# Attention blocks spread anew over the mixer's stages: more beside the first preparation and the middle stretch, fewer beside the chains

## The chip, the cores and the metric

One core of a Trainium2 chip runs the whole program. The metric is the device time of one execution in microseconds (us). Engines are named as in the profile: PE is TensorE's matmul stream and PEld its weight loads, DVE is VectorE, ACT is ScalarE, POOL is GpSimd, SP is SyncE, which issues DMAs; SPq is its queue.

## What is computed

One inference step of a two-layer backbone over 512 latent and 128 context tokens, 640 columns in all. Every layer is a SwiGLU, a token mixer and a second SwiGLU. What the change touches lies in the mixer of layer 0, which has two parts that do not depend on each other until the output projection:

```
p = h @ ab_w_in;  pa, pb = p[..., :ATTN_IN], p[..., ATTN_IN:]
oa = attention_mixer(pa, ...)     # 8 query heads, 2 kv heads, softmax
ob = rwkv_mixer(pb, ...)          # RWKV-7, one scan per direction
y  = concat([oa, ob]) @ ab_w_out
```

The attention is 20 jobs: 4 query heads of each kv head times 5 blocks of 128 queries. The first four blocks are latent queries (640 keys), the fifth is the context's (128 keys). The RWKV part runs on four pairs of heads (i = 0 to 3). Its scan over time is written in chunks of 64 tokens, ten chunks in each direction, with the inverse of a triangular matrix for every chunk, so that a scan is a chain of ten steps of small matmuls.

## The kernel before, in words

All of it is float32. Activations lie with channels on the partitions and the 640 tokens along the free axis.

`rwkv_attention` (L676) holds the mixer's second half, between the input projection and the output projection. Its work comes from five kinds of Python generators, each of which emits some instructions and then yields:

- `rwkv_prep(i)` (L971): loads r, k and v of pair i from DRAM (`rw_r`, `rw_k`, `rw_v`, one buffer each for r and k), makes decay, keys and rates for both directions on ACT, DVE and POOL (scan L1007, `ar` L1031, `kd` L1025, `bk` L1037 and L1038, `rr` L1066), then the chunk matrices `am` (matmuls into `ps_A`, mask L1054) and transposes `bt`. Counted as 22 yields.
- `tri_inverse` (L1209): the inverses of the 64 x 64 triangles. Four diagonal blocks go through DRAM (`invd`, L1222, L1229) to a substitution of many small DVE instructions (L1244, L1248), come back (`invx`, L1253, L1258), and are joined by 64 x 64 matmuls into `ps_n`. Counted as 16.
- `rwkv_chain(i)` (L1071): the ten steps, with matmuls into `ps_c` and `ps_yr`; at the end the final state goes out by SP (L1178). It needs the inverse of pair i. The tile `uv` has one buffer, so chains run one after the other. Counted as 12.
- `rwkv_out(i)` (L1180): group norm and gate, then a store to `od`. Counted as 4.
- `attention()` (L897): the 20 jobs. A job is two half-jobs, one of each kv head (`att_block`, L933), and the generator yields after each, 40 times in all. A half-job is scores into `ps_wide` (L941, L942; L944 for context), a maximum (DVE L947, L948), an exponential with its sum (ACT L950), a reciprocal (DVE L951), a scaling (ACT L952), transposes into `ps_pt` (PE L959) and their copies (ACT L961). The second half-job of a job adds the product with the values (PE L84 into `ps_pt`), a copy (ACT L929) and a store by SP to `od` (L930). The queries of the next job are loaded by SP (L73, `att_qin`) as soon as the one before it begins.

A half-job is called a block here. Blocks 0 to 39 come in the order of the jobs; in each group of ten, the last two are context blocks with 128 keys, called short, and the others, called long, have 640.

The function `take(rounds, n, *gens)` mixes them: in each of its rounds it advances every generator by its count over the rounds, and then the attention so that n blocks have been emitted by the last round, evenly spread. The eight calls are the stages: stage 1 is preparation 0; stage 2 inverse 0 with preparation 1; stage 3 chain 0 with inverse 1; stage 4 chain 1, preparation 2 and out 0; stage 5 out 1, inverse 2 and preparation 3; stage 6 inverse 3 and chain 2; stage 7 out 2 and chain 3; stage 8 out 3.

What the emission order sets: the program is built with a planner (`TileContext(nc, schedule_with_timeline_sim=True)`) that fixes the order of instructions on every engine's queue and takes the order of emission as a priority. On the chip each queue then runs in that fixed order; an instruction that waits holds up everything behind it on its queue. The loads that go through `load` (L71) are kept in emission order on SP, where the stores `od`, `invd`, `invx` and the final states are issued too.

Of the kernel before, what the change touches and what calls it, by code (L numbers as in the profile page):

```python
# [31 lines left out]
class K:  # L32
# [643 lines left out]
    def rwkv_attention(self):  # L676


        att = self.attention()
        mset = self.nc.gpsimd.memset  # L680

        self.rt = [self.mixb.tile([128, 2, 128], F32, name=f"rt{k}") for k in range(2)]
        for t in self.rt:
            mset(t[64:, 0], 0.0)
            mset(t[:64, 1], 0.0)

        self.st = [self.mixb.tile([128, 2, 2, 64], F32, name=f"st{k}") for k in range(4)]
        for t in self.st:
            for h in range(2):
                mset(t[64 - 64 * h:128 - 64 * h, :, h], 0.0)  # L690

        self.dx = [self.mixe.tile([128, 20, 64], F32, name=f"inv_d{k}") for k in range(2)]
        mset(self.dx[1].rearrange("p i t -> p (i t)"), 0.0)
        self.invd = [self.dram.tile([2, 80, 256], F32, name=f"invd{k}") for k in range(2)]
        self.invx = [self.dram.tile([2, 2, 80, 256], F32, name=f"invx{k}") for k in range(2)]
        un = [{} for _ in range(4)]

        def take(rounds, n, *gens):

            gens = [[g, 0.0, c] for g, c in gens]  # L700
            total, done = rounds, 0
            for step in range(rounds):
                for g in gens:
                    g[1] += g[2] / rounds
                    while g[0] is not None and (g[1] >= 1 or step == rounds - 1):
                        g[1] -= 1
                        try:
                            next(g[0])
                        except StopIteration:
                            g[0] = None  # L710
                while done < n * (step + 1) // rounds:
                    next(att, None)
                    done += 1

        prep = lambda i: (self.rwkv_prep(i, un[i]), 22)
        inv = lambda i: (self.tri_inverse(un[i]), 16)
        chain = lambda i: (self.rwkv_chain(i, un[i]), 12)
        out = lambda i: (self.rwkv_out(i, un[i]), 4)
        take(28, 5, prep(0))
        take(16, 4, inv(0), prep(1))  # L720
        take(12, 8, chain(0), inv(1))
        take(10, 7, chain(1), prep(2), out(0))
        take(12, 9, out(1), inv(2), prep(3))
        take(12, 5, inv(3), chain(2))
        take(12, 2, out(2), chain(3))
        take(4, 0, out(3))
        for _ in att:
            pass
# [1237 lines left out]
```

## Time and profile before

| | us |
|---|---|
| median of 3 runs | 3218.09 |
| lowest and highest | 3214.31, 3220.37 |
| the profiled execution, its own time | 3211.53 |
| span of the profile (first to last instruction) | 3209.8 |
| mean granted clock of TensorE, share of full | 0.949 |

The span is what the rows below are measured in, from its first instruction on. The mixer's stages lie between about 733 and 1237 us. The page's second part cuts the span into 40 slices of 80 us, one digit each, the busy share in tenths. Stages are cut in the trace by their own marks, for instance the last mask of `am` of a preparation or the store of a chain's final state.

### The profile page before, as it was taken

The numbers are of one execution on the slowest core, as the hardware profiler recorded it, in microseconds if no ns is written. First come the engines' busy times: TensorE is split into PE (matmuls) and PEld (weight loads), VectorE is DVE, ScalarE is ACT, GpSimd is POOL, SyncE is SP. The second block draws the span as 40 slices with busy tenths as digits, with TensorE's granted clock in tenths as the row PEclk, the third lists the DMA queues.
The fourth block names the chain that finished last, engine by engine and source line by source line (L and its number), as shares of the span: only waits on it lengthen the run. The fifth ranks groups of instructions, "written<-read, shape, count | busy, mean of one in ns | idle before, by whom it ended". The sixth has DMA issues, their size and how long they took to land.

```text
span 3209.8 us, 57218 instructions
## 1 busy us (share of the span) xinstructions
PE 2963.9 (92%) x23107; PEld 2763.7 (86%) x23107; DVE 1859.2 (58%) x3787; ACT 1182.7 (37%) x2443; POOL 694.7 (22%) x814
## 2 busy tenths in 40 slices
PE   7999999996888888999999999999987599999998
PEld 6999999884566667999999999999976499999998
DVE  5433348525656654854575876665678946633346
ACT  4422235424344434533333552222442245422223
POOL 1000005123112201533241322222223623000002
PEclk8999999997798898999999999999988899999998
DMA  6433335631111107354443454443478653432223
GB/s 225 139 132 119 109 104 183 214 128 45 18 29 33 21 14 194 108 168 138 152 150 124 139 174 148 148 153 109 139 154 242 240 178 100 162 108 79 69 90 112
DMA packets 370943, 408.55 MB, mean 127 GB/s; under 512 B 75258, under 2 KB 336695, under 8 KB 370423
## 3 DMA queue, kind: packets, MB, share of 16 engines
q1 hardware_dynamic: 356182, 365.93, 36.7%
q0 software_dynamic: 14496, 38.97, 4.2%
q8 instruction: 182, 2.98, 0.4%
q14 instruction: 83, 0.67, 0.1%
HBM read 358.79 MB, written 44.86 MB: 126 GB/s over the span
## 4 chain that ended last, share of the span: by engine, by line
PE 78%; DVE 8%; DMA 5%; POOL 3%; issue 3%; ACT 2%; SPq 1%; POOLq 0%; DVEq 0%; ACTq 0%
PE ps_h L439 10%; PE ps_h L440 10%; PE ps_h L441 10%; PE ps_wide L439 6%; PE ps_wide L440 6%; PE ps_wide L441 5%; PE ps_y L439 5%; PE ps_y L440 5%; PE ps_y L441 5%; PE ps_wide L274 2%; PE ps_n L84 1%; DVE s5x L1630 1%; PE ps_in L441 1%; PE ps_in L439 1%; PE ps_in L440 1%
## 5 line engine op out<-in xcount | busy, mean ns | idle before, releaser
L412 DVE TENSOR_TENSOR wlo<-w,whi 128x1024 fp32r<-128x1024 f32 (+2 forms) x574 | 574.9, 1008 | 387.9 <-ACT whi L411 380.7
L411 ACT CAST whi<-w 128x1024 fp32r<-128x1024 f32 (+2 forms) x576 | 482.9, 846 | 847.7 <-PE ps_h L440 277.7
L439 PE MATMUL ps_h<-hh,whi 128*128 128x320 f32 x2112 | 657.8, 312 | 6.5 <-ACT hh L356 2.4
L440 PE MATMUL ps_h<-hl,whi 128*128 128x320 f32 x2112 | 656.1, 311 | 0.3 <-DVE hl L357 0.3
L441 PE MATMUL ps_h<-hh,wlo 128*128 128x320 f32 x2112 | 655.3, 311 | 0.0
L439 PEld LDWEIGHTS ps_h<-hh,whi 128*128 128x128 f32 x2112 | 398.7, 189 | 13.2 <-ACT whi L411 4.5
L440 PEld LDWEIGHTS ps_h<-hl,whi 128*128 128x128 f32 x2112 | 398.1, 189 | 2.6 <-issue 1.5
L441 PEld LDWEIGHTS ps_h<-hh,wlo 128*128 128x128 f32 x2112 | 397.9, 188 | 1.2 <-issue 0.8
L440 PE MATMUL ps_y<-gl,whi 128*128 128x320 f32 x1056 | 325.9, 310 | 0.1
L441 PE MATMUL ps_y<-gh,wlo 128*128 128x320 f32 x1056 | 325.4, 310 | 0.0
L439 PE MATMUL ps_y<-gh,whi 128*128 128x320 f32 x1056 | 323.7, 311 | 1.4 <-ACT y L530 1.4
L439 PE MATMUL ps_wide<-hh,whi 128*128 128x320 f32 x912 | 288.6, 316 | 7.6 <-ACT pm L771 1.9
L440 PE MATMUL ps_wide<-hl,whi 128*128 128x320 f32 x912 | 285.9, 313 | 0.0
L441 PE MATMUL ps_wide<-hh,wlo 128*128 128x320 f32 x912 | 285.1, 313 | 0.4 <-DVE wlo L412 0.4
L373 POOL TENSOR_TENSOR ssy<-ssy,sq 128x320 f32<-128x320 f32 x84 | 95.5, 1137 | 559.2 <-ACT sq L372 556.7
L439 PEld LDWEIGHTS ps_y<-gh,whi 128*128 128x128 f32 x1056 | 197.1, 188 | 6.8 <-ACT y L530 2.5
L440 PEld LDWEIGHTS ps_y<-gl,whi 128*128 128x128 f32 x1056 | 198.2, 188 | 1.1 <-issue 0.5
L441 PEld LDWEIGHTS ps_y<-gh,wlo 128*128 128x128 f32 x1056 | 198.0, 188 | 1.1 <-issue 0.8
L439 PEld LDWEIGHTS ps_wide<-hh,whi 128*128 128x128 f32 x912 | 173.9, 191 | 15.3 <-issue 5.3
L481 DVE SCALAR_TENSOR_TENSOR g<-th,ps_h 128x320 f32<-128x320 f32 x159 | 77.1, 485 | 174.6 <-PE ps_h L441 174.1
L440 PEld LDWEIGHTS ps_wide<-hl,whi 128*128 128x128 f32 x912 | 173.3, 190 | 1.5 <-issue 0.9
L441 PEld LDWEIGHTS ps_wide<-hh,wlo 128*128 128x128 f32 x912 | 173.2, 190 | 1.0 <-DVE wlo L412 0.6
(464 smaller groups left out, 5588.0 us busy)
## 6 DMA issues: line engine op xcount, KB each, us to landing
w<-in_ffn_w_dram SPq DMA_DIRECT2D x120, 1024.0 KB
ada_w<-in_ada_w_dram SPq DMA_DIRECT2D x72, 1024.0 KB
w<-in_ffn_w_dram SPq DMA_DIRECT2D x112, 512.0 KB
w<-in_ab_w_in_dram SPq DMA_DIRECT2D x14, 1024.0 KB
s5cd<-s_work POOLq DMA_DIRECT2D x128, 64.0 KB, 2.4
s5bd<-s_st POOLq DMA_DIRECT2D x32, 256.0 KB, 3.5
s5bt<-s5bd SPq DMA_DIRECT2D x32, 256.0 KB
w<-in_s_w_out_dram SPq DMA_DIRECT2D x8, 1024.0 KB
```

The lines of the kernel that those rows point to most:

```text
L84: i = self.nc.tensor.matmul(**p).ins
L274: nc.tensor.matmul(ps[32 * g:32 * g + 32, :256], self.sc[:, 2 * t + k, :], w[:, k, g * 256:g * 256 + 256], start=(t + k == 0), stop=(2 * t ...
L373: nc.gpsimd.tensor_tensor(ss, ss, sq, op=OP.add)
L411: a = self.nc.scalar.copy(hi[:, :kt], s)
L412: v = (eng or self.nc.vector).tensor_tensor(lo[:, :kt], s, hi[:, :kt].bitcast(F32), op=OP.subtract)
L439: nc.tensor.matmul(o, hi[:, k], ah[k][half], start=(k == 0), stop=False)
L440: nc.tensor.matmul(o, hi[:, k], al[k][half], start=False, stop=False)
L441: self.last[0] = nc.tensor.matmul(o, lo[:, k], ah[k][half], start=False, stop=(k == kt - 1))
L481: nc.vector.scalar_tensor_tensor(g, t, 0.5, p3[:, :HALF], op0=OP.mult, op1=OP.mult)
L1630: V.tensor_tensor(dst, dst, t1, op=OP.add)
```

## The change

The second argument of seven `take` calls, which is the number of attention blocks emitted in that stage. The sum stays 40, and nothing else is edited.

```diff
-        take(28, 5, prep(0))
-        take(16, 4, inv(0), prep(1))
-        take(12, 8, chain(0), inv(1))
-        take(10, 7, chain(1), prep(2), out(0))
-        take(12, 9, out(1), inv(2), prep(3))
-        take(12, 5, inv(3), chain(2))
+        take(28, 8, prep(0))
+        take(16, 5, inv(0), prep(1))
+        take(12, 6, chain(0), inv(1))
+        take(10, 5, chain(1), prep(2), out(0))
+        take(12, 10, out(1), inv(2), prep(3))
+        take(12, 4, inv(3), chain(2))
         take(12, 2, out(2), chain(3))
         take(4, 0, out(3))
```

## Rows read from the trace of the kernel before

**Rows 1.** The page: its span, and PE's busy share in 40 slices of 80 us.

```profile
span 3209.8 us, 57218 instructions
...
PE   7999999996888888999999999999987599999998
```

**Rows 2.** Busy time by stage, stages 1 to 6, then 7 with 8 (PEclk: granted clock).

```profile
733.00:794.00 61.00, 42.83 (x228) 29.31 (x229) 33.61 (x56) 27.89 (x54) 18.46 (x11) 0.72 0.10 31
794.00:863.00 69.00, 53.52 (x533) 39.33 (x531) 47.90 (x125) 24.67 (x51) 17.55 (x10) 0.78 0.12 20
863.00:931.00 68.00, 57.86 (x894) 45.26 (x894) 39.73 (x144) 29.83 (x74) 5.30 (x4) 0.90 0.12 21
931.00:1018.00 87.00, 74.75 (x830) 56.92 (x827) 48.28 (x113) 39.29 (x98) 19.52 (x12) 0.86 0.11 34
1018.00:1111.00 93.00, 75.73 (x658) 55.84 (x655) 59.50 (x152) 40.08 (x86) 20.08 (x11) 0.82 0.13 27
1111.00:1176.00 65.00, 55.83 (x905) 45.10 (x904) 37.67 (x140) 23.10 (x62) 5.37 (x4) 0.87 0.11 18
1176.00:1237.00 61.00, 44.18 (x600) 33.41 (x600) 25.20 (x73) 22.80 (x59) 3.92 (x2) 0.88 0.24 66
```

**Rows 3.** The exponential's line L950 alone, stages 1 to 6; two instructions a block.

```profile
733.00:794.00 61.00, 5.88 (x12) 0.72 0.10 31
794.00:863.00 69.00, 3.09 (x8) 0.78 0.12 20
863.00:931.00 68.00, 7.50 (x15) 0.90 0.12 21
931.00:1018.00 87.00, 6.38 (x16) 0.86 0.11 34
1018.00:1111.00 93.00, 8.05 (x18) 0.82 0.13 27
1111.00:1176.00 65.00, 4.52 (x10) 0.87 0.11 18
```

**Rows 4.** The chain that ended last, from stage 3 into stage 4.

```profile
932.34 2.59 DMA out_dram<-s_out
...
937.02 3.21 DMA rw_k<-rwd
```

**Rows 5.** That chain by line, in stages 1, 3, 4, 5 and 6.

```profile
by line: PE ps_A L84 11.9%; PE ps_wide L941 10.4%; issue 7.2%; DVE ar L1031 7.0%; PE ps_pt L84 5.2%; DVE am L1054 4.8%; PE ps_w L849 4.3%; PE ps_bt L1059 3.8%; POOL kd L1040 3.4%; DVE bk L1037 3.3%; PE ps_hb L841 3.3%; POOL bk L1038 3.2%; P
...
by line: PE ps_n L84 12.8%; PE ps_pt L959 6.2%; DMA invd<-am 5.0%; DMA inv_d<-invx 4.9%; SPq L1258 4.5%; PE ps_wide L941 4.5%; PE ps_yr L1158 4.4%; DMA invx<-inv_x 4.0%; ACT att_p L950 3.9%; PE ps_c L1120 3.7%; DVE mx L947 3.5%; issue 3.4%;
...
by line: DMA rw_k<-rwd 7.6%; PE ps_A L84 7.5%; PE ps_wide L941 6.8%; PE ps_pt L84 4.4%; PE ps_hb L841 4.0%; DVE gi L1007 3.4%; PE ps_hs L822 3.4%; PE ps_bt L1059 3.4%; PE ps_yr L1158 3.2%; PE ps_pt L959 3.2%; PE ps_w L849 3.2%; DMA out_dram
...
by line: PE ps_n L84 11.7%; PE ps_A L84 8.6%; DVE am L1054 5.6%; PE ps_wide L941 4.5%; PE ps_pt L959 4.4%; DVE mx L947 4.4%; PE ps_w L849 4.2%; POOL am L1232 3.1%; PE ps_hb L841 3.1%; DVE inv_d L1283 2.8%; issue 2.8%; PE ps_pt L84 2.7%; SPq
...
by line: PE ps_n L84 22.3%; PE ps_yr L1158 5.9%; PE ps_pt L959 5.5%; PE ps_c L1145 4.5%; DMA invx<-inv_x 4.2%; PE ps_yr L1163 3.8%; DMA inv_a<-invd 3.5%; DMA inv_d<-invx 3.4%; DVE am L1283 3.4%; issue 3.2%; DVE inv_d L1283 3.2%; PE ps_c L11
```

**Rows 6.** Busy time summed over all stages, tiles ps_wide, att_p and pts.

```profile
sum 504.00, PE 53.06 PEld 27.09 DVE 28.66 ACT 35.99; mean PE 7.58 PEld 3.87 DVE 4.09 ACT 5.14
...
sum 504.00, PE 34.18 PEld 22.24 ACT 65.75; mean PE 4.88 PEld 3.18 ACT 9.39
...
sum 504.00, PE 26.67 PEld 21.68 ACT 27.08; mean PE 3.81 PEld 3.10 ACT 3.87
```

**Rows 7.** Timeline of stage 1: start, duration, instruction, idle before it and releaser.

```profile
780.91 1.23 PE L84 MATMUL ps_A<-ar,bk 64*128 64x128 f32 x8 [7.89 <-DVE bk L1037]
...
784.73 2.61 PE L84 MATMUL ps_A<-ar,bk 64*128 64x128 f32 x16
...
790.88 1.16 PE L84 MATMUL ps_A<-ar,bk 64*128 64x128 f32 x16
```

**Rows 8.** Waits on SP's queue, all stages: total us, times, longest.

```profile
SPq L930 <- ACT att_out L929: 110.0, 13, 22.3
```

## The prediction

> **What bounds the kernel now.** I read the page first. PE is busy nearly all the time outside the mixer of layer 0; the slices from 720 to 1280 us are the weak stretch, with digits of 6 to 9 [rows 1]. The change edits nothing outside that stretch, so the rest of the 3209.8 us span is taken as unchanged, and the whole question is what some 500 us do.
>
> The second view is the busy time by stage [rows 2]. Stages 1 and 2 leave PE idle most: 61 - 42.83 = 18.2 us and 69 - 53.52 = 15.5 us, and the granted clock is low there (0.72 and 0.78). Stages 3, 4 and 6, those with a chain, have PE busy for 85 to 86% at 0.86 to 0.90. Stage 5 is in between (81%, 0.82), with DVE at 59.50 of 93 us. No engine is full anywhere: each stage is a path of dependent steps that runs from engine to engine, with fixed queues, and attention is what stands between those steps.
>
> Do the blocks run where they are emitted? The exponential has two instructions a block, so the counts of its line are 6, 4, 7.5, 8, 9 and 5 blocks in stages 1 to 6 [rows 3], against 5, 4, 8, 7, 9 and 5 emitted. The planner stays within about one block of the emission. So the new numbers will be seen in the trace.
>
> Are the stages serial? The chain that ended last goes from the store of chain 0's final state (932.34, 2.59 us) to the load of preparation 2's k on the same queue (937.02, 3.21 us) [rows 4]. Preparation 2 can't start before chain 0 has ended. So a microsecond saved in stage 3 is passed on, and one lost in stage 1 too.
>
> **Which blocks move.** Emitted before, stage by stage: 0-4, 5-8, 9-16, 17-23, 24-32, 33-37, 38-39. After: 0-7, 8-12, 13-18, 19-23, 24-33, 34-37, 38-39. The short blocks are 8, 9, 18, 19, 28, 29, 38 and 39. Counted so, stage 1 gains three long blocks, stage 2 one short (it gives away 5, 6, 7 and receives 9 to 12), stage 3 loses two long, stage 4 one long and one short, stage 5 gains one long, stage 6 loses one long. Four long blocks and a short one leave the chains' stages and come into those without.
>
> **What a block is made of.** PE: 53.06 us of scores, 34.18 of transposes and 26.67 of products with the values, 113.9 us in all [rows 6]. With a short block counted as a quarter (an estimate: one key block of five, and fixed parts), these are 34 long ones, 3.35 us each. ACT: 65.75 + 27.08 = 92.8 us, 2.7 us each; DVE: 28.66 us, 0.84 each. A block also issues DMAs: each pair of blocks loads two query tiles and stores one `od` tile on SP. That queue has been held up by such stores for 110.0 us, 13 times [rows 8], mostly with nothing urgent behind them; a store that comes earlier stands ahead of preparation 1's loads and inverse 0's `invd`. POOL's queue has no instruction of a block.
>
> **What a block costs where it stands.** The bounds are nothing (all in idle time) and 3.35 us (all on the path). The nearest evidence between is the chain by line [rows 5], in which I add the attention's lines and divide by the blocks of the stage [rows 2, 3]:
>
> - Stage 1: 10.4 + 5.2 = 15.6% of 61 us is 9.5 us, over 6 blocks 1.6 us.
> - Stage 3: 6.2 + 4.5 + 3.9 + 3.5 = 18.1% of 68 us is 12.3 us, over 7.5 blocks 1.6 us.
> - Stage 4: 6.8 + 4.4 + 3.2 = 14.4% of 87 us is 12.5 us, over 8 blocks 1.6 us.
> - Stage 5: 4.5 + 4.4 + 4.4 + 2.7 = 16.0% of 93 us is 14.9 us, over 9 blocks 1.65 us.
> - Stage 6: 5.5% of 65 us is 3.6 us, over 5 blocks 0.7 us.
>
> The lines that the view cuts off are missing in all of them alike. A second witness: stages 3 and 6 hold the same other work, a chain and an inverse, and last 68 and 65 us with 7.5 and 5 blocks [rows 2, 3]; that is 1.2 us a block, inside the same bounds. I take the chain's prices, because they exist for every stage and the pair agrees within half a microsecond. Stage 2 takes stage 1's price, a quarter of it for a short block.
>
> **The sum.** Stage 1 +3 x 1.6 = +4.8; stage 2 +0.4; stage 3 -2 x 1.6 = -3.2; stage 4 -1.25 x 1.6 = -2.0; stage 5 +1.65; stage 6 -0.7. Together +0.9 us: the blocks cost about as much where they go as where they come from. The profiled execution took 3211.53 us, so 3212.4 by its measure; the median of the runs, 3218.09, stands 6.6 us above it, and I forecast 3219.0 by the median. A difference below 0.2%, some 6.4 us, is about what a measurement of this kernel can't tell from none.
>
> **Rival 1, faster: the idle time of stage 1 takes the blocks for nothing.** For it: PE waited 7.89 us in one piece before `ps_A` of the second direction [rows 7], with three blocks not yet emitted that would fill it (three long blocks are 10 us of PE against 18.2 us idle). And the 16 matmuls into `ps_A` right after took 2.61 us where the next 16 took 1.16 us; the granted clock was 0.72 over the stage, so much of it ran at the lower of the two levels, 1.2 GHz, after that wait. A filled gap gives back 1.45 us there. Beside chains a block is then worth its PE time times PE's busy share: stage 3 -2 x 2.85, stage 4 -1.25 x 2.9, stage 6 -2.9, stage 5 +2.7, stages 1 and 2 nothing but the -1.45. Sum -11 us: 3207. Against it: the queue of PE was in fixed order while it waited those 7.89 us, with a block's transposes standing behind `ps_A`; and during that wait DVE was the path, which blocks load too.
>
> **Rival 2, slower: in stage 1 the added blocks stand ahead of the path.** Preparation 0 is one chain of steps with nothing to overlap it but attention. If the queue order puts scores, transposes, maxima and stores ahead of ready steps, each block costs its whole 3.35 us in stages 1, 2 and 5 (+10, +0.8, +3.35), while stages 3, 4 and 6 return the pair's 1.2 us or less (-2.4, -1.5, -0.7): +9.5 us, 3227.6. It decides from about 3.0 us a block in stage 1 on: then the sum passes 6.4 us. For it: 15.6% of stage 1's chain is attention already. Against it: 1.6 us a block so far.
>
> **Rival 3, slower: the chains lose their fill and the clock.** With fewer blocks PE waits more between the steps of a chain, and runs its many small matmuls at the lower level. Stage 6, with 5 blocks, has 0.87 where stage 3 with 7.5 has 0.90, and stage 5 has 0.82 where stage 4 has 0.86 [rows 2, 3]. If stages 3 and 4 fall to those, 6% of 68 us and 8% of 87 us more run at half rate, and half of that is lost: 5.5 us, with the sum 6.4 us: 3224.5. The Trainium skill, page "TensorE: Matmul & The Clock Gate", section "Why this matters for your kernels", says to leave no idle gaps between bursts of matmuls, since PE falls to half rate; by that rule fill should not leave the chains, and equally should come into stage 1. The trace agrees for the gap in stage 1 [rows 7] and is thin for the chains, since five blocks cost stage 6 only 0.03 of clock.
>
> **Rival 4: the planner undoes it**, and blocks run where they ran. Then nothing changes. Rows 3 speak against it.
>
> **How the numbers follow.** Forecast 0.40, rival 1 0.30, rival 2 0.21, rival 3 0.06, rival 4 0.03. Faster is rival 1, 0.30; within 0.2% the forecast and rival 4, 0.43; slower rivals 2 and 3, 0.27. The range reaches from rival 1 less the 3 us by which runs differ, 3204, to rival 2 plus as much, 3231. Between cases of both signs the forecast's own range is 3212 to 3225.
>
> **What would show it.** Exponentials of about 8, 5, 6, 5, 10 and 4 blocks in stages 1 to 6. By the forecast stage 1 is 5 us longer than 61, stages 3 and 4 together some 5 us shorter than 155, stage 5 nearly 2 us longer than 93. Rival 1 leaves stage 1 at 61 or less, with a smaller wait before `ps_A` and a clock above 0.72. Rival 2 makes it over 70. Rival 3 shows in a clock under 0.87 in stage 3. I am wrong if the stages' differences don't add up to the change of the span, or if another part of the program moves by over 3 us.

## The result and the profile after

The change makes the kernel slower: a median of 3237.08 us (3236.42 to 3238.98, 4 runs) against 3218.39 us (4 runs), a ratio of 1.006 with the interval 1.0044 to 1.0076. That is 18.7 us, outside the forecast's range. The profiled execution after took 3238.98 us with a span of 3237.2 us, 27.4 us over the span of before [rows 1]. That is more than the medians show, because the profile of before was 6.9 us below its own median and this one 1.9 us above.

The page of the changed kernel, its span and PE's busy share in the 40 slices, answers to [rows 1]:

```profile
span 3237.2 us, 57222 instructions
...
PE   7999999997688787999999999999986689999998
```

The weak stretch is where it was. Next, busy time by stage, stages 1 to 6 and then 7 with 8, which answers to [rows 2] (columns: stretch, its length, busy time of PE, PEld, DVE, ACT and POOL, granted clock, DMA share, GB/s):

```profile
735.80:804.30 68.50, 51.76 (x271) 36.54 (x272) 37.22 (x65) 35.09 (x70) 18.85 (x11) 0.73 0.10 30
804.30:887.50 83.20, 55.16 (x543) 40.12 (x542) 51.65 (x129) 26.73 (x55) 18.89 (x10) 0.75 0.11 18
887.50:955.50 68.00, 55.07 (x892) 43.44 (x890) 36.10 (x140) 25.15 (x69) 5.35 (x4) 0.90 0.11 20
955.50:1039.90 84.40, 69.77 (x780) 52.93 (x781) 49.35 (x108) 35.67 (x84) 19.51 (x11) 0.86 0.11 33
1039.90:1136.70 96.80, 75.48 (x655) 54.57 (x655) 58.38 (x152) 42.24 (x89) 21.27 (x11) 0.81 0.12 26
1136.70:1197.20 60.50, 50.59 (x903) 40.43 (x901) 37.00 (x139) 21.22 (x58) 4.84 (x4) 0.94 0.12 19
1197.20:1260.20 63.00, 45.10 (x598) 34.11 (x599) 24.76 (x72) 22.40 (x58) 4.45 (x3) 0.83 0.24 63
```

Cut at the same marks to a tenth, the stages of before last 61.0, 69.2, 68.2, 88.2, 90.6, 65.9 and 60.5 us. So stage 1 grew by 7.5 us, **stage 2 by 14.0**, stage 5 by 6.2 and the last by 2.5; stage 3 gave 0.2 back, stage 4 3.8 and stage 6 5.4. Together +20.8 us. Stages 2 and 5 of the kernel before, at these marks:

```profile
793.80:863.00 69.20, 53.72 (x534) 39.46 (x532) 48.10 (x125) 24.67 (x51) 17.55 (x10) 0.78 0.12 20
...
1019.40:1110.00 90.60, 73.52 (x647) 54.41 (x646) 57.54 (x148) 39.47 (x84) 20.08 (x11) 0.81 0.13 27
```

In stage 2 PE is hardly busier (53.72 us before, 55.16 after). The 14 us are mostly waiting.

The stages' 20.8 us are not the 27.4 us of the span: 3.0 lie ahead of the mixer and 3.6 behind it, which the prediction named as a sign of being wrong. No edit touches the program there, and the stretch behind the mixer lasts from 1967 to 1980 us over the nineteen profiles. So 6.6 us are within what two profiles differ by, and say nothing of the change.

Did the blocks move as the diff says? The exponential's line alone, stages 1 to 6, answers to [rows 3] (columns: stretch, length, busy time of ACT with the count, two for a block):

```profile
735.80:804.30 68.50, 8.36 (x18) 0.73 0.10 30
804.30:887.50 83.20, 4.51 (x10) 0.75 0.11 18
887.50:955.50 68.00, 5.08 (x12) 0.90 0.11 20
955.50:1039.90 84.40, 4.91 (x10) 0.86 0.11 33
1039.90:1136.70 96.80, 9.04 (x20) 0.81 0.12 26
1136.70:1197.20 60.50, 3.53 (x8) 0.94 0.12 19
```

They did: 9, 5, 6, 5, 10 and 4 blocks. By kind, though, the blocks that ran differ from those emitted. Stage 1 has eight long and one short where it had six long, and stage 2 four long and one short where it had two of each.

In stage 1 the timeline of PE answers to [rows 7]:

```profile
787.65 2.07 PE L941 MATMUL ps_wide<-keys,att_qin 128*128 128x512 f32 x2 [5.85 <-ACT att_p L950]
...
790.08 2.24 PE L84 MATMUL ps_pt<-pts,vt 128*64 128x128 f32 x20
792.25 0.71 PE L84 MATMUL ps_A<-ar,bk 64*128 64x128 f32 x8
```

The wait of 7.89 us ahead of `ps_A` is gone; a block fills that place. But the block's own scores now wait 5.85 us for an exponential, and the stage as a whole is longer. On SP the stores held the queue nearly as before, as the waits of that queue show (columns: total us, times, longest), against [rows 8]:

```profile
SPq L930 <- ACT att_out L929: 117.1, 16, 22.8
```

What fills stage 2? PE's longest new wait there stands in front of the first joining matmul of inverse 0. The timeline of the kernel before shows the substitution that this matmul needs, and what came behind it (columns: start, duration, instruction, idle before it with its releaser):

```profile
799.53 0.17 DVE L1244 TENSOR_TENSOR inv_t<-inv_a,inv_x 80x14 f32<-80x14 f32 x1 [1.00 <-ACT inv_x L1237]
...
807.23 0.28 DVE L1248 TENSOR_TENSOR inv_x<-inv_x,inv_t 80x14 f32<-80x14 f32 x2
...
809.25 0.49 DVE L1005 TENSOR_SCALAR lw<-lw 128x640 f32<-128x640 f32 x1 [1.74 <-ACT lw L1004]
...
815.25 0.44 PE L84 MATMUL ps_n<-inv_d,am 64*64 64x64 f32 x2 [3.81 <-DMA inv_d<-invx]
```

The same stretch of the changed kernel:

```profile
809.93 0.17 DVE L1244 TENSOR_TENSOR inv_t<-inv_a,inv_x 80x14 f32<-80x14 f32 x1 [3.24 <-ACT inv_x L1237]
...
819.10 0.49 DVE L1005 TENSOR_SCALAR lw<-lw 128x640 f32<-128x640 f32 x1 [1.26 <-ACT lw L1004]
...
819.74 1.48 DVE L1007 TENSOR_TENSOR_SCAN gi<-reset,lw 128x640 f32<-128x640 f32 x1
...
823.14 0.16 DVE L951 RECIPROCAL mx<-mx 128x1 f32<-128x1 f32 x1 [1.02 <-ACT att_p L950]
...
823.81 2.31 POOL L1034 TENSOR_TENSOR ar<-rw_r,e 128x640 f32<-128x640 f32 x1 [11.60 <-ACT e L1014]
...
823.90 0.81 DVE L1031 SCALAR_TENSOR_TENSOR ar<-kkh,e 128x630 f32<-128x630 f32 x1
...
824.63 1.52 DVE L1244 TENSOR_TENSOR inv_t<-inv_a,inv_x 80x14 f32<-80x14 f32 x1
...
826.14 0.81 DVE L947 TENSOR_REDUCE mx<-ps_wide 128x1 f32<-128x640 f32 x1
...
826.88 0.16 DVE L1248 TENSOR_TENSOR inv_x<-inv_x,inv_t 80x14 f32<-80x14 f32 x1
...
834.31 0.44 PE L84 MATMUL ps_n<-inv_d,am 64*64 64x64 f32 x2 [8.65 <-DMA inv_d<-invx]
```

Read the substitution as one thing, from the first L1244 to the last L1248. Before, it ran from 799.53 to 807.51, 7.98 us, and preparation 1's `lw` and `gi` stood behind it. After, it runs from 809.93 to 827.04, 17.11 us, and `lw`, `gi`, `ar`, a block's reciprocal and maxima stand inside it, some of them waiting for ACT. It issues the same 56 instructions; the planner has put twelve others between them where there were four. The loads through DRAM follow from its end, so PE's wait grew from 3.81 to 8.65 us, and preparation 1's next `ps_A` matmuls stand behind that wait on PE's queue.

Inverse 2 in stage 5 has the same: its substitution lasts 18.29 us after, with fifteen others inside (12.48 us before, with nine), and PE's wait for it grew from 1.24 to 7.73 us:

```profile
1045.68 0.30 PE L84 MATMUL ps_n<-inv_d,am 64*64 64x64 f32 x2 [1.24 <-DMA inv_d<-invx]
...
1072.03 0.45 PE L84 MATMUL ps_n<-inv_d,am 64*64 64x64 f32 x2 [7.73 <-DMA inv_d<-invx]
```

### The profile page after: what moved, and what is told of

Its sections match the earlier page's. It is cut to its first block, busy times and chain, and to the rows that moved or that the text cites. A ratio compares the mean times of both kernels' runs of the same rounds, so it can differ in the third digit from the quotient of the medians.

```text
span 3237.2 us, 57222 instructions
## 1 busy us (share of the span) xinstructions
PE 2966.6 (92%) x23107; PEld 2765.3 (85%) x23107; DVE 1856.8 (57%) x3787; ACT 1185.6 (37%) x2445; POOL 696.0 (22%) x814
## 4 chain that ended last, share of the span: by engine, by line
PE 77%; DVE 9%; DMA 4%; POOL 3%; ACT 3%; issue 3%; SPq 1%; POOLq 0%; DVEq 0%; ACTq 0%
PE ps_h L439 10%; PE ps_h L440 10%; PE ps_h L441 10%; PE ps_wide L439 6%; PE ps_wide L440 6%; PE ps_wide L441 5%; PE ps_y L439 5%; PE ps_y L440 5%; PE ps_y L441 5%; PE ps_wide L274 2%; PE ps_n L84 1%; DVE s5x L1630 1%; POOL ssx L373 1%; PE ps_in L441 1%; PE ps_in L439 1%
```

## The experiments

**Theory A, order:** the loss comes from the substitutions being broken up on DVE's queue. **Theory B, weight:** it comes from what the added blocks themselves take in stages 1, 2 and 5. The table is the summary; the runs follow. Columns: ratio to the kernel before; length of stages 1, 2 and 5; length of the whole mixer; substitution of inverse 0 and of inverse 2 (first L1244 start to last L1248 end); PE's wait ahead of the first `ps_n` of inverse 0 and 2. Times in us; all columns but the ratio are read from one profile of each kernel, at the same marks. A ratio is against the kernel before run beside it; it need not be the quotient of two medians. A substitution is called whole where it lasts no more than 12.5 us, as both do in the kernel before, and broken where it lasts longer; what stands inside it differs by degrees.

| kernel | ratio | stage 1, 2, 5 | mixer | subst. 0, 2 | wait 0, 2 |
|---|---|---|---|---|---|
| before | 1 | 61.0, 69.2, 90.6 | 503.7 | 8.0, 12.5 | 3.8, 1.2 |
| changed | 1.0060 | 68.5, 83.2, 96.8 | 524.3 | 17.1, 18.3 | 8.7, 7.7 |
| e1_early | 1.0059 | 66.7, 86.9, 100.4 | 527.6 | 16.4, 18.1 | 8.6, 7.7 |
| e2_late | 1.0007 | 66.9, 70.2, 96.3 | 506.9 | 8.0, 12.2 | 3.9, 0 |
| e3_first | 1.0060 | 66.7, 81.6, 95.8 | 519.7 | 17.9, 17.1 | 15.1, 7.6 |
| e4_pin | 1.0060 | 68.7, 84.6, 95.5 | 523.9 | 13.1, 16.9 | 7.4, 7.6 |
| e5_behind | 1.0059 | 66.4, 77.8, 101.2 | 528.2 | 8.6, 23.6 | 1.1, 8.9 |
| e6_seven | 1.0031 | 63.0, 74.2, 91.5 | 505.4 | 8.1, 12.0 | 5.4, 0 |
| e7_four | 1.0010 | 58.2, 76.4, 91.5 | 513.8 | 12.1, 10.8 | 1.4, 4.1 |
| e8_second | 1.0024 | 61.0, 82.5, 97.1 | 513.6 | 8.0, 21.0 | 2.7, 9.7 |
| e9_behind02 | 1.0019 | 68.7, 78.3, 89.1 | 510.4 | 8.6, 11.9 | 1.1, 1.5 |
| e14_first_behind02 | 1.0004 | 68.4, 73.4, 86.3 | 510.2 | 8.7, 8.5 | 2.7, 1.5 |
| e15_behind2 | 1.0047 | 68.5, 88.8, 86.8 | 519.4 | 17.1, 8.4 | 8.7, 1.3 |
| e13_split | 0.9989 | 63.2, 79.4, 91.9 | 506.8 | 15.7, 10.7 | 7.3, 3.9 |
| e16_split2 | 1.0036 | 64.2, 69.7, 100.4 | 515.7 | 8.0, 17.6 | 4.0, 7.7 |
| e17_both | 1.0025 | 64.2, 76.9, 96.4 | 512.6 | 17.2, 17.2 | 7.8, 6.9 |
| e10_before_behind2 | 0.9989 | 63.2, 70.1, 88.4 | 503.8 | 8.0, 8.5 | 3.8, 0 |
| e11_chains | 0.9977 | 61.0, 69.3, 85.8 | 495.2 | 8.0, 8.0 | 3.9, 3.3 |
| e12_chains_behind2 | 0.9973 | 64.7, 69.5, 81.7 | 496.8 | 8.0, 8.0 | 3.8, 2.9 |

### Which part of the change

The first half alone (stages 1 to 4), the second half alone (stages 5 and 6), and three blocks moved from stage 2 to stage 1 with all else as before:

```diff
 e1_early: counts 8, 5, 6, 5, 9, 5, 2, 0
 e2_late:  counts 5, 4, 8, 7, 10, 4, 2, 0
 e3_first: counts 8, 1, 8, 7, 9, 5, 2, 0
```

> Block counts 8, 5, 6, 5, 9, 5, 2, 0: the change without its swap of one block between stages 5 and 6. Both theories put the loss into stages 1 and 2, where the trace after lost 7.5 and 14.0 us, and have stages 5 and 6 cancel (+6.0 and -5.4 us). Theory A (order: the inverse's substitution in stage 2 is broken up on DVE's queue) and theory B (weight: every block costs its work, about 3 us, outside the chains' stages, and nothing comes back beside chains): both 3234 to 3240, ratio 1.005 to 1.007. A ratio under 1.003 would say that the late swap is the cause.

> Block counts 5, 4, 8, 7, 10, 4, 2, 0: only the swap between stages 5 and 6. Both theories: within 2 us of before, 3216 to 3221, stage 5 some 3 to 6 us longer and stage 6 as much shorter. Slower by over 5 us would say that the late swap carries the loss.

> Block counts 8, 1, 8, 7, 9, 5, 2, 0: three blocks from stage 2 to stage 1, nothing else moved. Theory B (weight): stage 1 longer by 7 us, stage 2 shorter by about as much, since three blocks fewer stand there: total within 3 us of before. Theory A (order): stage 1 longer by 7 us; stage 2 depends on whether DVE's order still breaks up the substitution of inverse 0: if it does, the first matmul of the inverse comes 25 us after the diagonal blocks' landing instead of 16 us and the total is 8 to 16 us slower; if not, as theory B.

e1_early took 3234.14 us, ratio 1.0059 [1.004, 1.0078]: the whole loss. e2_late took 3217.77 us, 1.0007 [0.9994, 1.002]: none. e3_first took 3234.5 us, 1.006 [1.0043, 1.0077]: the whole loss again, though stages 1 and 2 together emit as many blocks as before and no chain loses one. The price that three blocks have in one stage rather than the next can hardly be 19 us when their PE work is 10; it needs a second mechanism.

### Mending the order in the changed kernel

First, preparation 1's `lw` and `gi` alone were put behind the substitution's last step:

```diff
-            nc.vector.tensor_scalar(lw, lw, 1.0, None, op0=OP.add)
-            gi = self.tmp("gi")
+            with (self.tc.issue_after(self.sub_last.ins) if (i, d) in ((1, 0),) else ExitStack()):
+                nc.vector.tensor_scalar(lw, lw, 1.0, None, op0=OP.add); gi = self.tmp("gi")
...
+                self.sub_last = nc.vector.tensor_tensor(x[:, d, s + 1:, :s], x[:, d, s + 1:, :s], t3, op=OP.add)
```

> The changed kernel, with the first scan of preparation 1 (its two DVE instructions, lw and gi) put behind the last step of inverse 0's substitution on DVE's queue. Theory A (order): the substitution ends some 8 us earlier after its start, as before the change, PE's wait of 8.65 us for the diagonal inverses shrinks to about 4, and 6 to 10 us come back: 3227 to 3231, ratio 1.003 to 1.004. Theory B (weight): the blocks in stage 2 cost what they cost, 3235 to 3239, ratio 1.005 to 1.007.

It took 3234.73 us, 1.006 [1.0037, 1.0083]. Theory A's expectation was missed, and the profile says why: the substitution still lasted 13.1 us, because a block's reciprocal, waiting for its exponential, and a maximum stood inside it. So all DVE work emitted after the substitution was queued behind its last step, first for inverse 0, then for inverses 0 and 2, later for inverse 2 alone:

```diff
-                            next(g[0])
+                            with queued(): next(g[0])
...
-                    next(att, None)
+                    with queued(): next(att, None)
...
+                self.sub_last = done if s == 14 and u["n"] in (0,) else self.sub_last; yield
```

Here `queued` is `issue_after` of the last L1248 step of the named inverse; e9_behind02 has `(0, 2)`, e15_behind2 `(2,)`, and e14_first_behind02 is e3_first with `(0, 2)`.

> The changed kernel, with all DVE work that is emitted after inverse 0's substitution (preparation 1's and the blocks') queued behind the substitution's last step, so that only two instructions of preparation 1 remain inside it. Theory A (order): the substitution takes 8 to 10 us again instead of 17.1, PE's wait for the diagonal inverses falls from 8.65 us to about 4, stage 2 falls from 83 us to 72 to 76 us: 3222 to 3229, ratio 1.001 to 1.003. Theory B (weight of the blocks): stage 2 stays over 80 us, 3233 to 3239, ratio 1.005 to 1.007.

> The changed kernel, with the DVE work emitted after the substitutions of inverse 0 and of inverse 2 queued behind the last step of each. Theory A (order): the substitution of inverse 2 falls from 23.6 us (with only inverse 0 so treated) or 18.3 (after) to under 12, stage 5 from 101 to 88 to 94 us, stage 2 stays near 78: the mixer 510 to 516 us instead of 524 to 528, in all 3218 to 3226, ratio 1.001 to 1.003. Theory B (weight): stage 5 stays over 96 us with its ten blocks, ratio 1.005 to 1.007.

> Three blocks moved from stage 2 to stage 1 (counts 8,1,8,7,9,5,2,0, as in e3_first, which took 1.006 of before), and the VectorE work that the substitutions of inverses 0 and 2 had inside them queued behind their last step. Theory A (order): what is left is the three blocks in stage 1 at some 1.6 us each less what stage 2 gives back, ratio 1.000 to 1.002. Theory B (weight): the blocks still run in stage 1, ratio 1.005 to 1.006 as in e3_first.

> The changed kernel; only inverse 2's substitution has its foreign VectorE work queued behind its last step, inverse 0's stays broken as the change leaves it (17.1 us). Theory A (the order costs at both places, in full): half of what e9_behind02 won back, some 3225 to 3230 us, ratio 1.003 to 1.0045. Theory C (a broken substitution costs at the end of the mixer only in stage 5; what stage 2 loses is mostly given back later, as e13_split suggests): nearly all that e9_behind02 won, 3217 to 3222 us, ratio 1.000 to 1.002. Theory B (weight): unchanged, 1.005 to 1.006.

e5_behind: 3232.39 us, 1.0059 [1.0036, 1.0081]. Stage 2 shrank from 83.2 to 77.8 us as theory A has it, but the planner laid stage 5 anew, inverse 2's substitution went to 23.6 us and stage 5 to 101.2. The loss had moved. The queueing holds back all DVE work emitted later, so a mended kernel differs in more than the inside of the substitution. e9_behind02, with both kept whole, took 3218.89 us, 1.0019 [1.0007, 1.003], with the change's own block counts. Its stage 2, PE's first `ps_n`, and stage 5, by stage and by timeline:

```profile
800.80:879.10 78.30, 57.19 (x544) 40.90 (x544) 52.55 (x132) 27.81 (x58) 18.14 (x10) 0.74 0.11 19
...
1029.40:1118.50 89.10, 72.65 (x656) 51.49 (x655) 59.76 (x153) 42.09 (x89) 21.31 (x11) 0.87 0.13 28
```

```profile
823.13 0.44 PE L84 MATMUL ps_n<-inv_d,am 64*64 64x64 f32 x2 [1.14 <-DMA inv_d<-invx]
```

The wait of 8.65 us is down to 1.14, and stage 5 lasts 89.1 us instead of 96.8. From 1.0060 to 1.0019 is about two thirds of the loss, some 13 us. (The same queueing behind inverse 2 makes the kernel before faster as well, 0.9989 in e10_before_behind2 below. Against that about 10 us of the loss are left, and the mend is worth half of it.) e14_first_behind02 makes it plainer: 3220.34 us, 1.0004 [0.9992, 1.0016], where the same three moved blocks cost 1.006 with the substitutions broken. Theory B, which expected no difference from e3_first, falls there. e15_behind2 mends only the second substitution: 3233.22 us, 1.0047 [1.0033, 1.0061]. With the change's counts the first one matters as well:

```profile
801.40:890.20 88.80, 61.72 (x543) 45.03 (x542) 51.61 (x128) 26.79 (x55) 19.02 (x10) 0.67 0.10 17
```

PE idles 27.1 us of stage 2, as in the changed kernel (28.0), against 21.1 in e9_behind02. That the stage is 5.6 us longer still than in the changed kernel goes with the clock: the same matmuls keep PE busy for 61.72 us at 0.67, for 55.16 at 0.75.

### Breaking the order in the kernel before

The reverse test leaves every block where it was and only holds the late steps of a substitution behind preparation work: inverse 0's from s = 10 behind preparation 1's first `gi`; inverse 2's from s = 13 behind preparation 3's first `ar`; and both, behind `ar`.

```diff
+                o = nc.vector.tensor_tensor(t3, xa[:, d, s, s + 1:][:, :, None].to_broadcast([80, n, s]),
...
+                if u["n"] == 0 and s == 10: self.held.append(o.ins)
...
+            z = nc.vector.tensor_tensor_scan(gi, self.reset, rv(lw), 0.0, op0=OP.mult, op1=OP.add)
+            if (i, d) == (1, 0):
+                for h in self.held:
+                    self.tc.add_manual_dep(h, z.ins.name, mybir.DependencyInfo(mybir.DependencyClass.NoSync, mybir.DependencyReason.DATA), reason="split")
```

> The kernel before with its own block counts; only the last steps of inverse 0's substitution are made to stand behind preparation 1's first scan gi on VectorE, so that waiting work of preparation 1 lies inside the substitution, as in the changed kernel. Theory A (order of VectorE's queue): the substitution of inverse 0 lasts 13 us or more (8.0 before), TensorE's wait for the inverse grows, and the kernel takes 6 to 12 us longer than before, ratio 1.002 to 1.004. Theory B (weight of the blocks executed in stages 1 and 2): no block has moved, so no difference, ratio 1.000 within 0.001.

> The kernel before with its block counts; the last steps of inverse 2's substitution are held behind preparation 3's first ar, which puts inside it the same VectorE work as the changed kernel has there. Theories A and C: the substitution lasts 17 us or more (12.5 before), stage 5 is 4 to 8 us longer and so is the kernel, ratio 1.0012 to 1.0025. Theory B: no block has moved, 1.000 within 0.001.

> The kernel before with its block counts; both substitutions broken, inverse 0's as in e13_split, inverse 2's as in e16_split2, so that VectorE's order inside both is nearly that of the changed kernel while the blocks stay where they were. If the order alone makes the loss (A): ratio 1.004 to 1.006. If only stage 5 counts (C): as e16_split2, 1.0012 to 1.0025. If the order costs only beside the blocks that the change put there (D, order and weight together): 1.000 to 1.002, with stage 2 longer and later stages shorter by as much.

e13_split: 3215.04 us, 0.9989 [0.9977, 1.0]. This is a miss for theory A. Its step came true, the substitution lasted 15.7 us and PE waited 7.3, and stage 2 was 10.2 us longer, but the end did not move. In its profile stages 2 and 6 read:

```profile
795.60:875.00 79.40, 57.96 (x534) 43.73 (x533) 48.27 (x125) 24.58 (x51) 17.55 (x10) 0.70 0.11 17
...
1119.80:1182.00 62.20, 52.32 (x912) 41.39 (x911) 38.23 (x142) 23.35 (x63) 5.35 (x4) 0.97 0.12 19
```

Stages 4, 6 and 7 gave back 3.4, 3.7 and 3.3 us against the profile of before, with stage 6 at a clock of 0.97 instead of 0.87. e16_split2 (stage 5 and PE's first `ps_n` of inverse 2):

```profile
1025.20:1125.60 100.40, 78.91 (x647) 58.60 (x646) 57.26 (x149) 39.58 (x84) 20.10 (x11) 0.75 0.12 24
```

```profile
1057.30 0.44 PE L84 MATMUL ps_n<-inv_d,am 64*64 64x64 f32 x2 [7.68 <-DMA inv_d<-invx]
```

It took 3227.15 us, 1.0036 [1.0023, 1.0049]: the order of stage 5 alone, with no block moved, costs about 11 us at the end, more than was expected. e17_both, both broken, took 3223.39 us, 1.0025 [1.0016, 1.0034], no more than the second alone. Its stage 2 shows the first break without a change of clock:

```profile
799.00:875.90 76.90, 53.42 (x533) 39.55 (x532) 48.12 (x124) 24.78 (x51) 17.68 (x10) 0.78 0.11 18
```

PE is as busy as before the change (53.72 us at 0.78) and idles 23.5 us instead of 15.5. e17_both came out as theory C of its expectation has it, not as A or D, but e15_behind2 missed C. None of these theories fits every run. So the order by itself makes 8 to 11 us with the blocks of before; a late inverse 0 adds to that only beside the change's blocks (e15_behind2 against e9_behind02, 1.0047 to 1.0019).

### How the loss depends on where blocks stand

```diff
 e6_seven:  counts 7, 2, 8, 7, 9, 5, 2, 0
 e7_four:   counts 4, 5, 8, 7, 9, 5, 2, 0
 e8_second: counts 5, 8, 6, 5, 9, 5, 2, 0
```

> Block counts 7, 2, 8, 7, 9, 5, 2, 0: two blocks from stage 2 to stage 1, one fewer than in the experiment with 8 and 1. In the program's fixed order inverse 0's substitution has three foreign DVE instructions inside it, as few as before the change (four), against more than ten with 8 and 1. Theory A (order): within 5 us of before, 3212 to 3221, ratio 0.999 to 1.0015. Theory B (weight): two thirds of the loss of 8 and 1, 3226 to 3230, ratio 1.0035 to 1.0045.

> Block counts 4, 5, 8, 7, 9, 5, 2, 0: one block from stage 1 to stage 2, the opposite direction. In the fixed order the substitution of inverse 0 now has seven foreign DVE instructions inside it, with preparation 1's first scan and a block's maximum among them. Theory A (order): the substitution takes 11 to 15 us instead of 8, and the total is 3 to 9 us slower, 3219 to 3225. Theory B (weight): one block less in stage 1 and one more in stage 2 cancel, 3213 to 3219.

> Block counts 5, 8, 6, 5, 9, 5, 2, 0: four blocks more in stage 2, taken from stages 3 and 4, with stage 1 as before; in the fixed order the substitution of inverse 0 is as before (four foreign instructions). Theory A (order): stage 2 longer by no more than the blocks' own share on the path, 4 to 7 us, stages 3 and 4 give back 2 to 4: 3217 to 3222, ratio 1.0005 to 1.002. Theory B (weight, 3 us a block outside the chains' stages and nothing back): 12 us slower, 3226 to 3230, ratio 1.0035 to 1.0045.

e6_seven: 3223.01 us, 1.0031 [1.0018, 1.0045], with both substitutions whole, so something besides their order costs here. It came out between the two expectations, nearer to B's. That it is the blocks' weight is not shown: stage 1, at 63.0 us, is within the spread of the kernels with five blocks, and stage 2 lost two long blocks and is 5.0 us longer. PE is busy there for 53.43 us at a clock of 0.66, before for 53.72 at 0.78, and idles 20.8 us instead of 15.5. e7_four, with a block taken out of stage 1 (58.2 us) and put into stage 2 (76.4), shows no clear difference: 3217.72 us, 1.001 [0.9998, 1.0022], as theory B expected, though the substitution grew to 12.1 us as theory A has it. e8_second puts four more blocks in stage 2 and takes them from the chains: 3220.31 us, 1.0024 [1.0004, 1.0043], a ratio again between the two expectations. Stage 2 was 82.5 us with inverse 0's substitution whole, 13.3 us for four blocks or 3.3 each, which is theory B's price; stage 5 was broken as well (21.0 us).

### The opposite of the change

If stage 5 is the dear place and chains take blocks cheaply, the counts should go the other way. The kernel before with inverse 2 kept whole, two blocks from stage 5 to stage 3, and both:

```diff
 e10_before_behind2: counts of before, queued behind inverse 2
 e11_chains:         counts 5, 4, 10, 7, 7, 5, 2, 0
 e12_chains_behind2: e11_chains, queued behind inverse 2
```

> The kernel before, with the DVE work emitted after inverse 2's substitution queued behind its last step. Theory A (order): the substitution takes 8 to 9 us instead of 12.5, stage 5 is 2 to 4 us shorter, 3211 to 3214, ratio 0.9985 to 0.9995. Theory B (weight): no difference, 0.9995 to 1.001, since the same blocks stand in the same stages.

> Block counts 5, 4, 10, 7, 7, 5, 2, 0: the opposite of the change, two blocks more beside chain 0 and two fewer beside preparation 3. By stages 3 of all runs so far, which last 65 to 70 us with four to eight long blocks, a block there costs under 1 us, and one in stages 2 and 5 about 3 us: stage 3 1 to 2 us longer, stage 5 5 to 6 us shorter, with the substitution of inverse 2 down to four foreign instructions: 3209 to 3213, ratio 0.998 to 0.9995. If a block weighs the same everywhere: 1.000.

> Block counts 5, 4, 10, 7, 7, 5, 2, 0 as well, and the DVE work emitted after inverse 2's substitution behind its last step. Theory A (order): 1 to 2 us better than without that, since only 2.5 us of foreign work are inside it already: 3207 to 3212, ratio 0.9975 to 0.999. Theory B: as without it.

e10_before_behind2: 3210.97 us, 0.9989 [0.9978, 1.0]. e11_chains: 3207.02 us, 0.9977 [0.9967, 0.9987]. e12_chains_behind2: 3206.58 us, 0.9973 [0.9961, 0.9985]. The last two beat both kernels and can't be told apart. Stages 3 and 5 of e11_chains:

```profile
863.10:934.20 71.10, 61.11 (x922) 48.03 (x920) 40.90 (x150) 33.73 (x85) 5.34 (x4) 0.90 0.12 22
...
1018.00:1103.80 85.80, 69.08 (x608) 50.42 (x607) 57.12 (x142) 34.78 (x73) 20.13 (x11) 0.78 0.13 27
```

Stage 3 is 2.9 us longer than before and stage 5 4.8 shorter. (Stages 3 and 4 together last 154.9 us, against 154.4 on average over the ten kernels with before's counts there.) In stage 5 the planner now keeps inverse 2's substitution at 8.0 us (12.5 before) without any queueing by hand. Which of the two, the blocks' weight or that order, carries the gain was not taken apart; e10_before_behind2, the order alone, has 0.9989.

## Why the prediction was wrong

**Stage 1, +4.8 forecast, +7.5 in the profile: the sum right within what one profile can tell, by some luck.** The kernels with five blocks emitted there show 61.0 to 66.9 us over nine profiles, mean 63.3; those with eight show 66.4 to 68.7 over eight, mean 67.8. That is 4.5 us. By emission it is three long blocks, 1.5 each against the 1.6 taken; but those that ran there are two long ones more, in five of the eight kernels with a short one, so some 2 us each. The count was too high and the price too low.

**Stage 2, +0.4 forecast, +14.0 measured: the step that failed, twice over.** The term was sized by counting emitted blocks: one short block more. In the executed count the stage has five blocks, four of them long, where before it had four, two of them long. At the 3.3 us each of e8_second, two long blocks more would be 6.6 us, not 0.4; PE's busy time grew by less, 1.4 us in the changed kernel and 3.5 in e9_behind02.

The second part is the order, which the term left out. PE's idle time tells it apart better than the length, which moves with the clock. PE idled 15.5 us of stage 2 before and 28.0 after; in e9_behind02, with the same blocks and the substitution whole, it idles 21.1 us. So 7 us of waiting go with the broken substitution, and 8 us in e17_both, where no block moved. The 5.6 us between 15.5 and 21.1 stay open: PE has two late waits in e9_behind02, 2.60 us ahead of a `ps_n` and 3.37 ahead of a `ps_A`. The changed kernel has them too, the kernel before doesn't, nor does e8_second with six long blocks there, and no run takes them away.

**Stages 3 and 4, -5.2 forecast, -4.0 measured.** The pair's sum fell from 156.4 to 152.4 us, close to the forecast, but part of that lies in the profile of before. Over the ten kernels with before's counts in these two stages the sum averages 154.4 us (152.6 to 156.6), over the seven with the change's counts 151.5 (149.9 to 155.1). That is 2.9 us for three and a quarter blocks, 0.9 each, not 1.6. e11_chains and e12_chains_behind2, with two blocks more in stage 3, have 154.9 and 153.1. The price in the chains is lower than the chain by line gave it, and its size stays within this spread.

**Stage 5, +1.65 forecast, +6.2 measured.** The added block itself cost nothing that shows there: with the second substitution queued as a whole, ten blocks last 89.1 us (e9_behind02) and 86.8 (e15_behind2), nine last 86.3 (e14_first_behind02) and 88.4 (e10_before_behind2). The broken substitution of inverse 2 made the waiting: PE idles 21 to 25 us of stage 5 in all eight kernels where it lasts 16.9 us or more, and 14 to 17 in the eleven where it lasts 12.5 or less. e16_split2 shows it without a moved block. The stage's length alone would mislead, since it moves with the clock too: e2_late has ten blocks, a whole substitution and 96.3 us, 79.94 of them busy PE at 0.77, and no loss at the end.

**Stage 6, -0.7 forecast, -5.4 measured.** Over all profiles the kernels with four blocks emitted there average 61.8 us and those with five 64.7, so a block there was worth 2.9 us, not 0.7.

**What the sum left out.** It priced blocks by where they stand and took the order of everything else as given. The planner lays every queue anew when the emission changes by a few blocks, and what it put between 56 dependent steps of some 0.2 us was not in any term. The prediction spoke of fixed queues in rivals 1 and 2, but for what the blocks do on the path of stage 1; that preparation 1's own steps could come to stand inside inverse 0's was in neither. Order is shown as a cause from both sides: mending it gives back 13 of 19 us (some 10, if the kernel before is mended too), and making it without a moved block costs 8 to 11. The 6 to 10 us that are left go with the blocks in stages 1 and 2, by the profiles alone; no run separates their weight from the waits that a new layout brings.

**The rivals.** Rival 1 (idle time takes the blocks) had its mark, the wait ahead of `ps_A` gone, and was wrong all the same: stage 1 grew, and its clock stayed at 0.73. Rival 2 had the right sign; its place was wrong: stage 1 did not pass 70 us. Its 3.35 us a block holds for stage 2 (e8_second, 3.3), not for stage 1. (Its threshold was worked out too high: with one price for its three stages the sum passes 6.4 us from 2.6 us a block on, not from 3.0.) Rival 3 was wrong: its mark was a clock under 0.87 in stage 3, and stage 3 has 0.90 with six blocks as with seven and a half. It leaned on the Trainium skill, page "TensorE: Matmul & The Clock Gate", section "Why this matters for your kernels", which says to leave no gaps between bursts of matmuls; the chains' clock did not follow the blocks here. In stage 2 it did: in e3_first, e6_seven and e14_first_behind02, which have no long block left there, it is 0.64 to 0.66 instead of 0.78. Rival 4 was wrong: the exponentials moved.

The page "Perfetto Trace Analysis", section "Identifying the Most-Contended Engine", also of the Trainium skill, says to optimize the engine with the highest occupancy first, and to judge TensorE not by its matmul busy share but by MFU (its arithmetic as a share of the peak) and the busy share of its weight loads. In stage 2 weight loads are busy for 40.12 us and DVE for 51.65, so by that page DVE comes ahead of them. The measurement agrees on the place: PE's wait went when the edit held back work on DVE's queue alone. It was DVE's order that counted, not its load, which was as high after the mend (52.55 us in e9_behind02).

**What stays open.** Why 10 us lost in stage 2 cost nothing at the end in e13_split, and little in e17_both, is not settled. Later stages ran shorter there, some at a higher clock, but the runs don't show which leads. Nor does one profile of a kernel separate 3 us in a stage: stage 1 of e2_late, whose instructions there are those of before, lasted 66.9 us and before's 61.0.

## What to carry to other kernels

Before filler work is moved into a stage, look there for long runs of small dependent instructions, and ask which waiting instruction a planner could now put between them: here the kernel with three moved blocks stood at 1.0004 with those runs kept whole and at 1.006 with them broken. Read the new order on each queue, not only where the filler itself went. A loss read from a stage must be tested at the end of the kernel, by mending it and by making it alone; here, with no block moved, one of the two breaks cost its full price and the other nothing.

## What the runs showed of the hardware

The same work at another clock: stage 6 holds 912 matmuls in before, e13_split and e17_both, and lasted 65.9 us at a granted clock of 0.87 (PE busy 56.76 us), 64.1 at 0.89 (55.23) and 62.2 at 0.97 (52.32). PE's idle time was the same in all three, 8.9 to 9.9 us, so the 3.7 us between the longest and the shortest went with the clock, as much as a moved block or two is worth.

A DVE step can be held until a POOL instruction ends. The substitution's step of 80x14 elements, 0.17 us elsewhere, took 1.52 us at 824.63 in the changed kernel and ended at 826.14; POOL's `ar`, started at 823.81, ended at 826.11, after 2.31 us (1.53 at 774.89 in the kernel before). Over the nineteen profiles ten steps of a substitution lasted more than 0.8 us. Each overlaps one POOL instruction and ends 0.03 to 0.06 us after it. This is some 1.4 us of the 9.1 by which inverse 0's substitution grew. No run took the POOL work away.
